# Moving half of the retention's projections beside the scans, a new order of the block inverses, and tokens loaded first

## The chip, the cores and the metric

The kernel runs on one core of one Trainium2 chip. The metric is the device time of one execution in microseconds (us). PE is TensorE (its weight loads are listed apart as PEld), DVE is VectorE, ACT is ScalarE, POOL is GpSimd; SP is SyncE, whose queue issues most of the DMA transfers.

## What is computed

Two transformer blocks follow each other on 1024 tokens of width 1024. Only the front of the first one is touched. There the tokens and 256 context tokens are normalised, modulated, and projected by `w_in` into two groups of columns: 2560 for a retention (q, k, v and two gates, 512 columns each) and 1920 for an RWKV part (r, k, v and low-rank terms). Cut to what matters:

```python
h = rms_norm(x, g_pre_mix) * (1.0 + sc1) + sh1
hc = rms_norm(ctx, g_pre_mix) * (1.0 + csc1) + csh1
u, uc = h @ w_in, hc @ w_in
ret_lat, _ = retention_group(u[..., :RET_COLS], uc[..., :RET_COLS], need_ctx)
rw = depthwise_conv(u[..., RET_COLS:], conv_w)
rwkv_lat, _ = rwkv_group(rw, rwc, ...)          # rwkv7_scan, forward and backward
lat = jnp.concatenate([ret_lat, rwkv_lat], axis=-1) @ w_out
```

`rwkv7_scan` is a recurrence over tokens, S = S * w_t + (S a_t) b_t + v_t k_t. The kernel computes it by chunks of 64 tokens, which takes the inverse of a triangular 64x64 matrix for each chunk, head and direction.

## The kernel before, in words

Python code writes the instructions; a scheduler then orders them on each engine by program order and by when it expects them to be ready, before the kernel runs. So a later part of the program may run beside an earlier one as far as its buffers are free; on the chip each engine goes through its list in order.

`phase_mod` (L147) loads 8 MB of modulation weights in eight transfers (L169) and makes the modulation columns (L171 to L181). `phase_h` (L227) loads the ten token tiles of 128 (L238), in groups of 4, 4 and 2, normalises them (L239, L240), transposes them on PE (L245), modulates them (L250, L252) and splits them in a high and a low part, hTh and hTl (L255, L256).

`phase_in` (L264) makes everything that the scans and the retention read, and writes it to DRAM. `project` (L326) gives the units of one block of 128 RWKV columns: up to three, by 512, 512 and 256 tokens, each with 24 matmuls; its result goes to Ud (L344). `retained` (L347) gives the units of 256 retention columns: one for each two token tiles, with 48 matmuls of 256 columns, whose result is stored in RD (L363). Each matmul is done three times, high by high, high by low and low by high (`mm3`, L106). `Weights.piece` (L74) loads a piece of weights (L90) and splits it on ACT (L91) and DVE or POOL (L92). The list `cols` (L566) holds the ten retained blocks: k, v, q and two gates f and b, for the first half of the heads and then for the second.

For each of four pairs of heads and for three token blocks, `prep` (L382) convolves r, k, v and builds the factors FA, FB and the triangular matrix L, which it stores in Ld (L500). The loop at L570 sets `prep` off in stages and puts projection units between the stages: those of the next pair, and of `cols` 0, 1, 2 to 3 and 4 to 6 for the four pairs. `tri(g)` (L502) inverts the 32x32 diagonal blocks of 128 matrices at once, one in each partition, row by row from the last: a product on DVE (L515) and a sum along the rows (L517). It is called for pair p-1 while pair p is prepared, for the context matrices (g = 4) in the last pair, and for pair 3 behind the loop (L598). The results go to Td (L524). Behind it stand the units of `cols` 7 to 9 (L599).

`phase_chain` (L603) does the scans: for each pair five groups, one of context chunks and four of latent chunks; a group does four chunks in each direction. For each direction come the scores (L684, L694), two sets of transposes (L701, L705), small products (L712, L713, L722, L731), two larger ones (L739, L752) and GQ (L757). Then four steps carry the state S (L777, L781, L786). Results are stored in Yd (L799). It reads some 24 tiles a group through SP. `phase_retention` (L828), with buffers from `ret_setup` (L802), does for each half of the heads some preparation (KV) and eight token blocks, whose results go to LatD (L932). Each second token block is followed by a part of `phase_mod2` (L184), which loads weights through POOL (L199) and sums on DVE (L203, L205). `phase_out` (L937) begins with the gates and the weights `w_out`.

The loop of units and preparations, and the end of phase_in:

```python
cols = [retained(*a, hh) for hh in range(2) for a in (("k", 512, 10), ...)]
for p in range(NPAIR):
    fill = pair(p + 1) if p < 3 else []
    for c in cols[(0, 1, 2, 4)[p]:(1, 2, 4, 7)[p]]:
        fill += c
    ...
W.lo_pool = True
tri(3)
for f in cols[7] + cols[8] + cols[9]:
    f()
```

Of the kernel before, what the change touches and what calls it, by code (L numbers as in the profile page):

```python
# [16 lines left out]
OP = mybir.AluOpType  # L17
# [129 lines left out]
def phase_mod(E, A):  # L147
# [8 lines left out]
    with tc.tile_pool(name="modp", bufs=1) as pool, tc.tile_pool(name="modps", bufs=1, space=PSUM) as pp:  # L156
# [7 lines left out]
        nc.vector.tensor_copy(E.cs.rearrange("p a k -> p (a k)"), cps[:, :2 * KD])  # L164
        rows = pool.tile([2, 4, 512], F32, name="modrows")
        ps = pp.tile([P, 512], F32, name="modps")
# [60 lines left out]
def phase_h(E, A):  # L227

    nc, tc = E.nc, E.tc
    E.hTh = E.hpool.tile([P, KD, TA], F32R, name="hTh")  # L230
    E.hTl = E.hpool.tile([P, KD, TA], F32R, name="hTl")
    with tc.tile_pool(name="php", bufs=3, side="right") as pool, tc.tile_pool(name="phps", bufs=3, space=PSUM, side="right") as pp:
        for g0, gn in ((0, 4), (4, 4), (8, 2)):
            xs = []
            for t in range(g0, g0 + gn):
                x = pool.tile([P, D], F32, tag="x", bufs=8, name=f"xin{t}")
                src = A.x[0, t * P:(t + 1) * P, :] if t < 8 else A.ctx[0, (t - 8) * P:(t - 7) * P, :]
                nc.sync.dma_start(x, src)  # L238
                r = row_norm(E, pool, x, f"n1_{t}")  # L239
                nc.vector.tensor_scalar(x, x, r, None, op0=OP.mult)  # L240
                xs.append(x)
            for k in range(KD):
                ps = pp.tile([P, 512], F32, tag="tp", name=f"htp{g0}_{k}")
                for i, x in enumerate(xs):
                    nc.tensor.transpose(ps[:, i * P:(i + 1) * P], x[:, k * P:(k + 1) * P], E.ident)  # L245
                n = gn * P
                c = 0 if g0 < 8 else 1
                f = pool.tile([P, 512], F32, tag="hf", name=f"hf{g0}_{k}")
                if k % 3 == 2:
                    nc.scalar.activation(f[:, :n], ps[:, :n], AF.Identity, scale=E.s1[:, k, c:c + 1], bias=E.mod[:, k, c:c + 1])  # L250
                else:
                    nc.vector.tensor_scalar(f[:, :n], ps[:, :n], E.s1[:, k, c:c + 1], E.mod[:, k, c:c + 1],  # L252
                                            op0=OP.mult, op1=OP.add)
                hi, lo = (a[:, k, g0 * P:g0 * P + n] for a in (E.hTh, E.hTl))
                nc.scalar.copy(hi, f[:, :n])  # L255
                (nc.vector if k % 2 else nc.gpsimd).tensor_sub(lo, f[:, :n], hi)  # L256
# [6 lines left out]

def phase_in(E, A):  # L264

# [8 lines left out]
                     (A.rwkv_a0, A.rwkv_k_k, A.rwkv_k_a, A.rwkv_r_k)])  # L274
    W0F, W0B, A0, KK, KA, RK = (lambda p, o=o: vec[:, o + p:o + p + 1] for o in (0, 4, 8, 12, 16, 20))
# [13 lines left out]
    Ud = [dt(f"Ud{m}", [P, TA + 4]) for m in range(16)]  # L289
# [3 lines left out]
    with ExitStack() as st:  # L293
        wp = st.enter_context(tc.tile_pool(name="inW", bufs=1))
        ep = st.enter_context(tc.tile_pool(name="inE", bufs=3))
        up = st.enter_context(tc.tile_pool(name="inU", bufs=1))
        tp = st.enter_context(tc.tile_pool(name="inT", bufs=1))
        rp = st.enter_context(tc.tile_pool(name="inR", bufs=1))
        pp = st.enter_context(tc.tile_pool(name="inP", bufs=4, space=PSUM))
        p2 = st.enter_context(tc.tile_pool(name="inQ", bufs=3, space=PSUM))  # L300
        W = Weights(E, wp, "inW", 128, 4, 3, 5)
# [24 lines left out]
        def project(m, blks):  # L326

            hold = []

            def unit(bi):  # L330
                if not hold:
                    hold.extend(W.full(w_in[:, R0 + CONV_COLS[m]:R0 + CONV_COLS[m] + P], P))
                t0, n, _ = TBLK[bi]
                ps = pp.tile([P, 512], F32, tag="pj", name=f"u{m}_ps{bi}")
                for k in range(KD):
                    mm3(nc, ps[:, :n], hold[k][0], hold[k][1], E.hTh[:, k, t0:t0 + n], E.hTl[:, k, t0:t0 + n], k == 0, k == KD - 1)
                ev = ep.tile([P, 514], F32, tag="ev", name=f"u{m}_{bi}")
                o = 0 if bi == 1 else 1
                w = n + (2 if bi == 2 else 1)
                for z in ((0,), (512,), (0, 257))[bi]:  # L340
                    nc.gpsimd.memset(ev[:, z:z + 1], 0.0)
                nc.scalar.copy(ev[:, o:o + n], ps[:, :n])  # L342
                d0 = (0, 513, 1026)[bi]
                nc.sync.dma_start(Ud[m][:, d0:d0 + w], ev[:, :w])  # L344
            return [lambda bi=bi: unit(bi) for bi in blks]

        def retained(n_, col, nt, hh):  # L347
# [4 lines left out]
            def unit(t0):  # L352
                if not hold:
                    hold.extend(W.full(w_in[:, col + c0:col + c0 + 256], 256, kper=2))
                ps = pp.tile([P, 512], F32, tag="pj", name=f"R{n_}{hh}_{t0}")
# [146 lines left out]
        def tri(g):  # L502
# [32 lines left out]

        for m, blks in ((12, (0, 1, 2)), (13, (0, 1, 2))):
            for f in project(m, blks):
                f()
# [31 lines left out]
        for p in range(NPAIR):  # L570
# [3 lines left out]
            for c in cols[(0, 1, 2, 4)[p]:(1, 2, 4, 7)[p]]:  # L574
                fill += c
# [23 lines left out]
        for f in cols[7] + cols[8] + cols[9]:  # L599
            f()  # L600


def phase_chain(E, A):  # L603
# [5 lines left out]
    with ExitStack() as st:  # L609
        ld = st.enter_context(tc.tile_pool(name="chL", bufs=2))  # L610
        wk = st.enter_context(tc.tile_pool(name="chW", bufs=2))
        cst = st.enter_context(tc.tile_pool(name="chC", bufs=1))
        ps_sc = st.enter_context(tc.tile_pool(name="chS", bufs=1, space=PSUM))
        ps_tr = st.enter_context(tc.tile_pool(name="chT", bufs=1, space=PSUM))
        ps_md = st.enter_context(tc.tile_pool(name="chM", bufs=2, space=PSUM))
        ps_ch = st.enter_context(tc.tile_pool(name="chX", bufs=2, space=PSUM))
        msk = cst.tile([P, 2, 2, 2, C], F32, name="scmask")
        nc.sync.dma_start(msk, E.consts["scmask"])

        PT4 = cst.tile([P, NPAIR, 20, 2, 2], F32, name="PT4")  # L620
        nc.vector.memset(PT4, 0.0)
        for p in range(NPAIR):
            for d in range(2):
                nc.vector.tensor_copy(PT4[0:64, p, :, d, 0], E.PT[0:64, p, d, :])
                nc.vector.tensor_copy(PT4[64:128, p, :, d, 1], E.PT[64:128, p, d, :])

        FAs = [cst.tile([P, G, 4, C], F32, name=f"FAb{i}") for i in range(4)]
        for t in FAs:
            nc.gpsimd.memset(t, 0.0)
        IRs = [cst.tile([P, G, 2, C], F32, name=f"IRb{i}") for i in range(4)]  # L630
        for t in IRs:
            nc.vector.tensor_copy(t[0:64, :, 0, :], E.ident[0:64, 0:64].unsqueeze(1).to_broadcast([64, G, C]))
            nc.vector.tensor_copy(t[64:128, :, 1, :], E.ident[64:128, 64:128].unsqueeze(1).to_broadcast([64, G, C]))

        TDs = [cst.tile([P, G, 2, C], F32, name=f"TDb{i}") for i in range(4)]
        for t in TDs:
            nc.gpsimd.memset(t, 0.0)
# [1772 lines left out]
def first(E, A):  # L2410
# [118 lines left out]
```

## Time and profile before

| | us |
|---|---|
| median of three runs | 4141.37 |
| lowest, highest | 4128.83, 4142.38 |
| the profiled execution | 4133.8 |
| its span, first to last instruction | 4132.0 |
| PE busy with matmuls | 3779.7 (91%) |
| PE busy with weight loads | 3133.2 (76%) |
| DVE busy | 2814.2 (68%) |
| ACT busy | 2127.7 (51%) |
| POOL busy | 825.2 (20%) |

The profiled execution lies between the runs. The stretch that the change touches is the first 1260 us; what follows is the output projection, the experts and the second block. A share over the whole span is a mean over stages with different limits, so the sections below go by stages.

### The profile page before, as it was taken

How to read it: one execution, taken by the hardware profiler on the slowest of the kernel's cores; microseconds unless marked ns; L12 is line 12 of the kernel's file. 1: busy time of each engine (PE TensorE's matmuls, PEld its weight loads, DVE VectorE, ACT ScalarE, POOL GpSimd, SP SyncE). 2: the span in 40 equal slices, each digit the busy share in tenths (PEclk: the TensorE clock that was granted, in tenths of full speed). 3: DMA queues.
4: the chain of work that ended last, by engine and by line, in shares of the span. 5: the costliest groups of instructions: out<-in, count | busy, mean ns of one | idle time of the engine just before them, and what ended most of it. 6: DMA issues, size and time to landing. Idle time of an engine off the chain costs nothing. (4 is left out here: it accounts for less than half of the span.)

```text
span 4132.0 us, 61749 instructions
## 1 busy us (share of the span) xinstructions
PE 3779.7 (91%) x23138; PEld 3133.2 (76%) x23138; DVE 2814.2 (68%) x4777; ACT 2127.7 (51%) x3389; POOL 825.2 (20%) x1054
## 2 busy tenths in 40 slices
PE   7988887998997879999969999999998999999998
PEld 4877886777875647777747788888886777788876
DVE  3578787776776578888865513676644356799987
ACT  3443322332323347777758712666653244688876
POOL 2333324233224120000010001222210022221111
PEclk7999998998998989999989999999999999899999
DMA  6555455455445379999851122111115425899998
GB/s 229 169 168 163 138 153 142 109 135 129 112 115 177 129 295 374 382 371 385 319 171 46 50 66 66 44 37 42 47 62 167 142 79 204 324 384 386 382 381 303
DMA packets 503961, 782.78 MB, mean 189 GB/s; under 512 B 199697, under 2 KB 334811, under 8 KB 502507
## 3 DMA queue, kind: packets, MB, share of 16 engines
q1 hardware_dynamic: 430314, 631.77, 43.8%
q0 software_dynamic: 40816, 138.37, 11.3%
q10 hardware_dynamic: 32528, 8.66, 0.9%
q8 instruction: 184, 3.01, 0.3%
q14 instruction: 119, 0.97, 0.1%
HBM read 646.28 MB, written 132.43 MB: 188 GB/s over the span
## 5 line engine op out<-in xcount | busy, mean ns | idle before, releaser
L2262 DVE TENSOR_TENSOR m2l<-m2r,m2h 128x1024 fp32r<-128x1024 f32 x380 | 449.6, 1222 | 53.0 <-ACT m2h L2261 48.6
L1195 DVE TENSOR_TENSOR m1l<-m1r,m1h 128x2048 fp32r<-128x2048 f32 x189 | 427.2, 2289 | 72.5 <-ACT m1h L1194 70.6
L2261 ACT CAST m2h<-m2r 128x1024 fp32r<-128x1024 f32 x384 | 394.0, 1050 | 86.5 <-PE m2g L109 34.6
L1194 ACT CAST m1h<-m1r 128x2048 fp32r<-128x2048 f32 x192 | 362.1, 1914 | 111.3 <-PE gu L109 82.6
L108 PE MATMUL m2g<-m2l,m2thx 128*128 128x512 f32 x512 | 202.7, 396 | 1.8 <-DVE m2l L2262 1.3
L107 PE MATMUL m2g<-m2h,m2thx 128*128 128x512 f32 x512 | 202.9, 405 | 0.3 <-ACT m2h L2261 0.3
L109 PE MATMUL m2g<-m2h,m2tlx 128*128 128x512 f32 x512 | 201.5, 394 | 0.0
L108 PE MATMUL gu<-m1l,xh 128*128 128x512 f32 x512 | 199.7, 395 | 0.0
L109 PE MATMUL gu<-m1h,xl 128*128 128x512 f32 x512 | 199.1, 395 | 0.0
L107 PE MATMUL gu<-m1h,xh 128*128 128x512 f32 x512 | 182.4, 397 | 12.7 <-ACT xh L60 8.3
L515 DVE TENSOR_TENSOR tripr<-triN,triX 128x1 f32<-128x1 f32 (+30 forms) x155 | 131.9, 851 | 19.5 <-POOL triX L511 15.9
L107 PE MATMUL apqk<-atW_hi,hT2h 128*128 128x256 f32 x512 | 145.1, 283 | 0.0
L108 PE MATMUL apqk<-atW_lo,hT2h 128*128 128x256 f32 x512 | 144.7, 283 | 0.0
L109 PE MATMUL apqk<-atW_hi,hT2l 128*128 128x256 f32 x512 | 144.7, 283 | 0.0
L107 PE MATMUL u_ps<-hTh,inW_hi 128*128 128x512 f32 (+1 forms) x336 | 127.1, 378 | 2.6 <-ACT u L342 1.5
L2314 POOL DMA_INDIRECT out_dram<-m2y,did x32 | 68.9, 2154 | 302.5 <-ACT m2y L2313 302.5
L108 PE MATMUL u_ps<-hTl,inW_hi 128*128 128x512 f32 (+1 forms) x336 | 124.4, 370 | 0.0
L109 PE MATMUL u_ps<-hTh,inW_lo 128*128 128x512 f32 (+1 forms) x336 | 124.1, 370 | 0.0
L107 PEld LDWEIGHTS gu<-m1h,xh 128*128 128x128 f32 x512 | 95.0, 188 | 37.0 <-ACT xh L60 10.7
L108 PEld LDWEIGHTS gu<-m1l,xh 128*128 128x128 f32 x512 | 96.4, 188 | 27.0 <-DVE m1l L1195 7.4
L1216 POOL DMA_INDIRECT accd<-y,idx x16 | 29.1, 1819 | 435.2 <-ACT y L1215 400.1
L108 PEld LDWEIGHTS m2g<-m2l,m2thx 128*128 128x128 f32 x512 | 96.8, 189 | 24.8 <-DVE m2l L2262 6.1
(1215 smaller groups left out, 11720.3 us busy)
## 6 DMA issues: line engine op xcount, KB each, us to landing
m2r<-in_w_gate_up_dram SPq DMA_DIRECT2D x128, 1024.0 KB
m1r<-in_w_gate_dram SPq DMA_DIRECT2D x64, 1024.0 KB
m1r<-in_w_up_dram SPq DMA_DIRECT2D x64, 1024.0 KB
m1r<-in_w_down_dram SPq DMA_DIRECT2D x64, 1024.0 KB
m2r<-in_w_down_dram SPq DMA_DIRECT2D x64, 1024.0 KB
inW_raw<-in_w_in_dram SPq DMA_DIRECT2D x72, 256.0 KB
m2w<-in_w_mod_dram POOLq DMA_DIRECT2D x32, 512.0 KB, 4.7
luW_raw<-in_w_in_dram SPq DMA_DIRECT2D x24, 512.0 KB
```

The source lines that it names most:

```text
L107: nc.tensor.matmul(ps, lh, rh, start=start, stop=False)
L108: nc.tensor.matmul(ps, lh, rl, start=False, stop=False)
L109: nc.tensor.matmul(ps, ll, rh, start=False, stop=stop)
L515: nc.vector.tensor_mul(pr[:, :m, :m], N[:, j, j + 1:].unsqueeze(1).to_broadcast([P, m, m]), X[:, j + 1:, j + 1:].rearrange("p s t -> p t s"))
L1194: nc.scalar.copy(hi, raw)
L1195: (nc.gpsimd if i < 3 else nc.vector).tensor_sub(lo, raw, hi)
L1216: nc.gpsimd.indirect_dma_start(out=E.accd, out_offset=bass.IndirectOffsetOnAxis(ap=E.idx[:, e:e + 1], axis=0), in_=y, in_offset=None, comp ...
L2261: nc.scalar.copy(hi, raw[:, j])
L2262: (nc.gpsimd if i in (0, 2) else nc.vector).tensor_sub(lo, raw[:, j], hi)
L2314: nc.gpsimd.indirect_dma_start(out=E.x4d, out_offset=bass.IndirectOffsetOnAxis(ap=col, axis=0), in_=y, in_offset=None, compute_op=OP.add)
```

## The change

The tokens are loaded and normalised by a class `Tokens` in three separate steps, and a new function `start` sets their order: the first group's loads stand ahead of the modulation's weights, the weights of the projections 12 and 13 ahead of the second group's loads, and the blocks of these projections between the token groups.

`tri` goes by columns instead of rows: for each column s from the last it multiplies column s of N with row s of X (an outer product) and adds it to the rows above.

The last pair's preparation gets only `cols[4]` beside it. The units of `cols` 5 to 9 (22 of them, the second half of the heads) are returned by `phase_in`, and `first` puts two of them behind each of the first eleven groups of the scans. For this `phase_chain` becomes a generator. Pools are laid on two sides of the memory, so that the scans' buffers and those of the projections are there at once; the projections have two PSUM buffers (inP2) in that time instead of four. The retention's buffers follow when the eleven groups are written.

```diff
+def start(E, A):
+    with tc.tile_pool(name="php", bufs=3, side="right") as pool, tc.tile_pool(name="phps", bufs=3, space=PSUM, side="right") as pp:
+        h = Tokens(E, A, pool, pp)
+        phase_mod(E, A, lambda: h.load(0))
+        low = [E.in_project(m, (None, 0, 1, 2)) for m in (12, 13)]
+        for u in low:
+            u[0]()
+        h.load(1)
+        h.norm(0)
+        h.turn(0)
+        h.load(2)
+        h.norm(1)
+        h.turn(1)
+        for u in low:
+            u[1]()
+        h.norm(2)
+        h.turn(2)
+        for u in low:
+            u[2]()
+            u[3]()
...
-            for j in range(B - 2, -1, -1):
-                m = B - 1 - j
-                pr = rp.tile([P, B - 1, B - 1], F32, tag="tP", name=f"tripr{g}_{j}")
-                nc.vector.tensor_mul(pr[:, :m, :m], N[:, j, j + 1:].unsqueeze(1).to_broadcast([P, m, m]),
-                                     X[:, j + 1:, j + 1:].rearrange("p s t -> p t s"))
-                nc.vector.tensor_reduce(X[:, j, j + 1:], pr[:, :m, :m], axis=AX.X, op=OP.add)
+            for s in range(B - 1, 0, -1):
+                m = B - s
+                pr = rp.tile([P, 16 * 16], F32, tag="tP", name=f"tripr{g}_{s}")[:, :s * m].rearrange("p (j t) -> p j t", t=m)
+                nc.vector.tensor_mul(pr, N[:, :s, s:s + 1].to_broadcast([P, s, m]),
+                                     X[:, s:s + 1, s:].to_broadcast([P, s, m]))
+                nc.vector.tensor_add(X[:, :s, s:], X[:, :s, s:], pr)
...
-        for m, blks in ((12, (0, 1, 2)), (13, (0, 1, 2))):
-            for f in project(m, blks):
-                f()
...
-            for c in cols[(0, 1, 2, 4)[p]:(1, 2, 4, 7)[p]]:
+            for c in cols[(0, 1, 2, 4)[p]:(1, 2, 4, 5)[p]]:
                 fill += c
...
         W.lo_pool = True
         tri(3)
-        for f in cols[7] + cols[8] + cols[9]:
-            f()
+        return sum(cols[5:], [])
...
+                yield
+    return run()
...
-        with tc.tile_pool(name="hp", bufs=1) as E.hpool:
-            with tc.tile_pool(name="pssm", bufs=1, space=PSUM) as E.ps_small:
-                phase_mod(E, A)
-                phase_h(E, A)
-                phase_in(E, A)
+        with ExitStack() as st:
...
+            start(E, A)
+            last = phase_in(E, A)
+            wide.close()
+            E.in_pools = E.in_pools[:2] + (ent(tc.tile_pool(name="inP2", bufs=2, space=PSUM, side="right")),)
+            cs = ExitStack()
+            run = phase_chain(E, A, cs)
+            for i, f in enumerate(last):
+                if i % 2 == 0:
+                    next(run)
+                f()
         with ExitStack() as E.rst:
-            E.rps = E.rst.enter_context(tc.tile_pool(name="reP", bufs=2, space=PSUM))
+            E.rps = E.rst.enter_context(tc.tile_pool(name="reP", bufs=2, space=PSUM, side="right"))
             tabs = ret_setup(E)
-            phase_chain(E, A)
+            for _ in run:
+                pass
+            cs.close()
             phase_retention(E, A, tabs, phase_mod2(E, A))
```

## Rows read from the trace of the kernel before

**Rows 1.** Windows by stage: PE, PEld, DVE, ACT, POOL busy, granted clock, DMA.
```profile
256.00:370.00 114.00, 102.70 (x717) 86.89 (x716) 94.24 (x156) 40.51 (x76) 43.14 (x71) 0.96 0.54 159
370.00:478.00 108.00, 96.28 (x749) 85.63 (x748) 86.14 (x146) 36.11 (x62) 36.58 (x54) 0.94 0.54 160
478.00:609.00 131.00, 109.97 (x935) 102.97 (x935) 119.25 (x198) 35.22 (x61) 41.26 (x51) 0.91 0.44 131
609.00:697.00 88.00, 67.32 (x541) 66.31 (x539) 63.61 (x99) 15.69 (x22) 26.70 (x29) 0.92 0.55 143
697.00:1260.00 563.00, 514.19 (x5257) 422.70 (x5257) 394.30 (x1041) 172.20 (x456) 175.80 (x229) 0.91 0.49 124
```

**Rows 2.** Windows for the tile tripr alone (the inverses): DVE busy, clock, DMA.
```profile
478.00:609.00 131.00, 79.27 (x121) 0.91 0.44 131
...
sum 441.00, DVE 209.55; mean DVE 52.39
```

**Rows 3.** Waits of PE and DVE, 256 to 609 us: total, times, longest.
```profile
PE ssi L438 <- DVE invb L433: 21.8, 5, 6.2
...
DVE L L492 <- PE psl L490: 19.0, 4, 13.5
```

**Rows 4.** Window with projections alone on PE, columns as in rows 1.
```profile
600.00:650.00 50.00, 50.00 (x419) 50.00 (x418) 38.44 (x55) 12.70 (x19) 14.05 (x13) 1.00 0.67 172
```

**Rows 5.** Timeline of SP and PE from the last projections to the scans.
```profile
636.37 38.63 SPq L363 DMA_DIRECT2D RDf<-Ref  x4
...
685.65 0.58 SPq L660 DMA_DIRECT2D FAb<-FA  x1
...
697.27 1.09 PE L857 MATMUL kTp<-ident,kt 128*128 128x128 f32 x4 [15.10 <-issue]
...
707.38 1.86 PE L694 MATMUL psc<-FAb,FB 128*128 128x128 f32 x7
```

**Rows 6.** Stores of the scans (Yd) and the retention (LatD): first and last.
```profile
L799 SPq DMA_DIRECT2D Yd<-yst x32: 320/378/716, 770.5 to 1256.2; - x32
L932 POOL DMA_DIRECT2D LatD<-gs x16: 582/619/635, 766.8 to 1243.5; - x16
```

**Rows 7.** Timeline of PE in one latent group of the scans.
```profile
1159.78 1.11 PE L739 MATMUL pw<-AT,TDb 128*128 128x128 f32 x8
1161.78 1.09 PE L752 MATMUL pg<-UT,W 64*64 64x128 f32 x16 [0.23 <-ACT W L741]
...
1165.26 0.59 PE L684 MATMUL psc<-FAb,FB 128*128 128x256 f32 x2
1165.69 0.38 PE L777 MATMUL pc<-S,GQ 128*128 128x128 f32 x2
...
1166.31 0.44 PE L777 MATMUL pc<-S,GQ 128*128 128x128 f32 x2
```

**Rows 8.** Timeline at the start: token loads, last modulation vector, first projection.
```profile
17.43 8.00 SPq L238 DMA_DIRECT2D xin<-in_x_dram  x8
30.59 0.17 DVE L181 SCALAR_TENSOR_TENSOR s<-s,c 128x16 f32<-128x16 f32 x1
64.94 0.77 PE L107 MATMUL u_ps<-hTh,inW_hi 128*128 128x512 f32 x1
```

**Rows 9.** Groups of DVE by form, 95 to 690 us: busy us, mean ns.
```profile
L470 DVE TENSOR_TENSOR FBt<-ic,ei 128x512 f32<-128x512 f32 x16 | 11.0, 685 | 0.0
L515 DVE TENSOR_TENSOR tripr<-triN,triX 128x961 f32<-128x961 f32 x5 | 9.6, 1926 | 0.1
L517 DVE TENSOR_REDUCE triX<-tripr 128x31 f32<-128x961 f32 x5 | 5.8, 1153 | 0.1
L470 DVE TENSOR_TENSOR FBt<-ic,ei 128x256 f32<-128x256 f32 x8 | 3.3, 418 | 0.0
```

**Rows 10.** Waits of PE's weight loads, 1254 to 1420 us.
```profile
PEld mo L107 <- ACT wohi L1047: 7.9, 2, 5.6
```

**Rows 11.** Waits, 1100 to 1260 us.
```profile
POOL m2w L199 <- DVE m2a L203: 29.1, 6, 11.8
```

More of the change, by code (lines that the diff above doesn't have):

```diff
@@ L144, in setup, with phase_mod @@
     nc.vector.memset(E.ones_col, 1.0)
-def phase_mod(E, A):
+def phase_mod(E, A, rows_first):
     nc, tc = E.nc, E.tc
@@ L155, in phase_mod @@
                              A.norm_gains[0, 0].rearrange("(r p) -> r p", p=P)])
-    with tc.tile_pool(name="modp", bufs=1) as pool, tc.tile_pool(name="modps", bufs=1, space=PSUM) as pp:
+    with tc.tile_pool(name="modp", bufs=1) as pool:
         crow = pool.tile([2 * KD, P], F32, name="crow")
@@ L164, in phase_mod @@
         nc.vector.tensor_copy(E.cs.rearrange("p a k -> p (a k)"), cps[:, :2 * KD])
+        rows_first()
         rows = pool.tile([2, 4, 512], F32, name="modrows")
-        ps = pp.tile([P, 512], F32, name="modps")
+        ps = E.in_pools[2].tile([P, 512], F32, tag="pj", name="modps")
         for k in range(KD):
@@ L224, in bc_row @@
     return t
[L227 to L256, printed above, removed]
@@ new lines, with __init__, load, norm @@
+class Tokens:
+    GROUPS = ((0, 4), (4, 4), (8, 2))
+    def __init__(self, E, A, pool, pp):
+        self.E, self.A, self.pool, self.pp = E, A, pool, pp
+        E.hTh = E.hpool.tile([P, KD, TA], F32R, name="hTh")
+        E.hTl = E.hpool.tile([P, KD, TA], F32R, name="hTl")
+        self.xs = {}
+    def load(self, g):
+        A, (g0, gn) = self.A, self.GROUPS[g]
+        for t in range(g0, g0 + gn):
+            x = self.xs[t] = self.pool.tile([P, D], F32, tag="x", bufs=8, name=f"xin{t}")
+            src = A.x[0, t * P:(t + 1) * P, :] if t < 8 else A.ctx[0, (t - 8) * P:(t - 7) * P, :]
+            self.E.nc.sync.dma_start(x, src)
+    def norm(self, g):
+        g0, gn = self.GROUPS[g]
+        for t in range(g0, g0 + gn):
+            x = self.xs[t]
+            r = row_norm(self.E, self.pool, x, f"n1_{t}")
+            self.E.nc.vector.tensor_scalar(x, x, r, None, op0=OP.mult)
+    def turn(self, g):
+        E, nc, pool = self.E, self.E.nc, self.pool
+        g0, gn = self.GROUPS[g]
+        for k in range(KD):
+            ps = self.pp.tile([P, 512], F32, tag="tp", name=f"htp{g0}_{k}")
+            for i in range(gn):
+                nc.tensor.transpose(ps[:, i * P:(i + 1) * P], self.xs[g0 + i][:, k * P:(k + 1) * P], E.ident)
+            n = gn * P
+            c = 0 if g0 < 8 else 1
+            f = pool.tile([P, 512], F32, tag="hf", name=f"hf{g0}_{k}")
+            if k % 3 == 2:
+                nc.scalar.activation(f[:, :n], ps[:, :n], AF.Identity, scale=E.s1[:, k, c:c + 1], bias=E.mod[:, k, c:c + 1])
+            else:
+                nc.vector.tensor_scalar(f[:, :n], ps[:, :n], E.s1[:, k, c:c + 1], E.mod[:, k, c:c + 1],
+                                        op0=OP.mult, op1=OP.add)
+            hi, lo = (a[:, k, g0 * P:g0 * P + n] for a in (E.hTh, E.hTl))
+            nc.scalar.copy(hi, f[:, :n])
+            (nc.vector if k % 2 else nc.gpsimd).tensor_sub(lo, f[:, :n], hi)
@@ L261, with in_project, project, unit @@
 CONV_COLS = [0, 128, 256, 384, 512, 640, 768, 896, 1024, 1152, 1280, 1408, 1536, 1600, 1728, 1856]
+def in_project(E, A, pools):
+    nc = E.nc
+    R0 = 2560
+    E.in_pools = wp, ep, pp = pools
+    E.Ud = [E.dram.tile([P, TA + 4], F32, name=f"Ud{m}") for m in range(16)]
+    E.in_W = W = Weights(E, wp, "inW", 128, 4, 3, 5)
+    def project(m, blks, hold=None):
+        hold = [] if hold is None else hold
+        def unit(bi):
+            if not hold:
+                hold.extend(W.full(A.w_in[0][:, R0 + CONV_COLS[m]:R0 + CONV_COLS[m] + P], P))
+            if bi is None:
+                return
+            t0, n, _ = TBLK[bi]
+            ps = pp.tile([P, 512], F32, tag="pj", name=f"u{m}_ps{bi}")
+            for k in range(KD):
+                mm3(nc, ps[:, :n], hold[k][0], hold[k][1], E.hTh[:, k, t0:t0 + n], E.hTl[:, k, t0:t0 + n], k == 0, k == KD - 1)
+            ev = ep.tile([P, 514], F32, tag="ev", name=f"u{m}_{bi}")
+            o = 0 if bi == 1 else 1
+            w = n + (2 if bi == 2 else 1)
+            for z in ((0,), (512,), (0, 257))[bi]:
+                nc.gpsimd.memset(ev[:, z:z + 1], 0.0)
+            nc.scalar.copy(ev[:, o:o + n], ps[:, :n])
+            d0 = (0, 513, 1026)[bi]
+            nc.sync.dma_start(E.Ud[m][:, d0:d0 + w], ev[:, :w])
+        return [lambda bi=bi: unit(bi) for bi in blks]
+    E.in_project = project
+def start(E, A):
+    nc, tc = E.nc, E.tc
+    with tc.tile_pool(name="php", bufs=3, side="right") as pool, tc.tile_pool(name="phps", bufs=3, space=PSUM, side="right") as pp:
[17 more added lines that the diff above has]
+            u[3]()
 def phase_in(E, A):
@@ L274, in phase_in @@
                      (A.rwkv_a0, A.rwkv_k_k, A.rwkv_k_a, A.rwkv_r_k)])
+    E.pss.close()
     W0F, W0B, A0, KK, KA, RK = (lambda p, o=o: vec[:, o + p:o + p + 1] for o in (0, 4, 8, 12, 16, 20))
@@ L288, in phase_in @@
     E.SGd = [dt(f"SGd{d}", [P, T]) for d in range(2)]
-    Ud = [dt(f"Ud{m}", [P, TA + 4]) for m in range(16)]
+    Ud = E.Ud
     E.RD = {n: dt(f"RD{n}", [TA if n in "kv" else T, 512]) for n in "qkvfb"}
@@ L293, in phase_in @@
     with ExitStack() as st:
-        wp = st.enter_context(tc.tile_pool(name="inW", bufs=1))
-        ep = st.enter_context(tc.tile_pool(name="inE", bufs=3))
+        wp, ep, pp = E.in_pools
         up = st.enter_context(tc.tile_pool(name="inU", bufs=1))
         tp = st.enter_context(tc.tile_pool(name="inT", bufs=1))
-        rp = st.enter_context(tc.tile_pool(name="inR", bufs=1))
-        pp = st.enter_context(tc.tile_pool(name="inP", bufs=4, space=PSUM))
+        rp = st.enter_context(tc.tile_pool(name="inR", bufs=1, side="right"))
         p2 = st.enter_context(tc.tile_pool(name="inQ", bufs=3, space=PSUM))
-        W = Weights(E, wp, "inW", 128, 4, 3, 5)
+        W, project = E.in_W, E.in_project
         lw = up.tile([P, 512], F32, name="lora_w2")
@@ L324, in phase_in @@
         AL = up.tile([P, TA], F32, name="AL")
[L326 to L345, printed above, removed]
         def retained(n_, col, nt, hh):
@@ L608, in phase_chain @@
     E.Yd = E.dram.tile([P, NPAIR, 2, 16, C], F32, name="Yd")
[L609 to L637, printed above, removed]
@@ new lines, in phase_chain @@
+    ld = st.enter_context(tc.tile_pool(name="chL", bufs=2))
+    wk = st.enter_context(tc.tile_pool(name="chW", bufs=2))
+    cst = st.enter_context(tc.tile_pool(name="chC", bufs=1))
+    ps_sc = st.enter_context(tc.tile_pool(name="chS", bufs=1, space=PSUM))
+    ps_tr = st.enter_context(tc.tile_pool(name="chT", bufs=1, space=PSUM))
+    ps_md = st.enter_context(tc.tile_pool(name="chM", bufs=2, space=PSUM))
+    ps_ch = st.enter_context(tc.tile_pool(name="chX", bufs=2, space=PSUM))
+    msk = cst.tile([P, 2, 2, 2, C], F32, name="scmask")
@@ new lines, in phase_chain @@
+    nc.sync.dma_start(msk, E.consts["scmask"])
+    PT4 = cst.tile([P, NPAIR, 20, 2, 2], F32, name="PT4")
+    nc.vector.memset(PT4, 0.0)
+    for p in range(NPAIR):
+        for d in range(2):
+            nc.vector.tensor_copy(PT4[0:64, p, :, d, 0], E.PT[0:64, p, d, :])
+            nc.vector.tensor_copy(PT4[64:128, p, :, d, 1], E.PT[64:128, p, d, :])
+    FAs = [cst.tile([P, G, 4, C], F32, name=f"FAb{i}") for i in range(4)]
+    for t in FAs:
+        nc.gpsimd.memset(t, 0.0)
+    IRs = [cst.tile([P, G, 2, C], F32, name=f"IRb{i}") for i in range(4)]
@@ L638, in phase_chain, with run @@
+    for t in IRs:
+        nc.vector.tensor_copy(t[0:64, :, 0, :], E.ident[0:64, 0:64].unsqueeze(1).to_broadcast([64, G, C]))
+        nc.vector.tensor_copy(t[64:128, :, 1, :], E.ident[64:128, 64:128].unsqueeze(1).to_broadcast([64, G, C]))
+    TDs = [cst.tile([P, G, 2, C], F32, name=f"TDb{i}") for i in range(4)]
+    for t in TDs:
+        nc.gpsimd.memset(t, 0.0)
+    def run():
         un = 0
```

11 lines of the change are left out of this document (9 added, 2 removed).

## The prediction

> **What bounds the kernel now.** I read the stretch that the change touches, the first 1260 us, by stages [rows 1], then what each stage waits for, then single durations. In the three stages where pairs 1 to 3 are prepared (256 to 370, 370 to 478, 478 to 609 us) the reader is to see DVE, not PE: it is busy 94.24 of 114, 86.14 of 108 and 119.25 of 131 us. Of that the block inverses alone take 79.27 in the third, and 209.55 us over all five, 42 each [rows 2]. PE's own wait there is for DVE: 21.8 us for invb [rows 3]. After 609 us come what is left of the retention's projections, dense on PE (50.00 of 50 us, 419 matmuls, so 119 ns each [rows 4]), then a gap of 15.1 us on PE and only at 707 us the first scores of the scans [rows 5]. From there the scans' 20 groups and the retention's 16 token blocks run side by side to 1256 and 1243.5 us [rows 6].
>
> That last stage has two readings. PE's matmul rows are busy 514.19 of 563 us, 91%; its weight loads are busy 422.70, 75% [rows 1], where the dense projections show 50.00 of 50 in both [rows 4]. So by matmuls there is room for 49 us of projections beside the scans, by weight loads for 140. I take the second: a pair of 256-column matmuls is drawn 0.59 us long, yet the next begins 0.43 later; overlapping tails fill the matmul row [rows 7]. The Trainium skill ("Perfetto Trace Analysis", Identifying the Most-Contended Engine) says the same: matmul busy share is no measure of PE's headroom, weight-load share is; by it the 125 us moved below would fit, by the other reading they would not, and that is a rival below. The trace agrees with it in the dense stretch.
>
> **The change, part by part.**
>
> *Start (tokens first).* Now the last modulation vector is ready at 30.6 us and the first projection starts at 64.94 [rows 8]. Afterwards four token tiles (2 MB) go ahead of the modulation's weights; eight took 8.00 us to issue, so the modulation comes 4 to 6 us later, but the first four norms are done under it, and the weights of the projections 12 and 13 and their block 0 no longer wait for the two other token groups. Their issues (4 weight loads, 6 stores) only move ahead on SP's queue, past the constants' small loads. Bounds 5 and 17 us, taken: 12 us gained, nearer the upper end since one whole token group (some 11 us of 35 for three) leaves the path.
>
> *Inverses.* Now 31 steps of a product and a sum over m x m, 42 us each. Afterwards 31 steps of a product and an addition over s(32-s) elements, 5456 in all instead of 10416. The longest old product took 1.93 us for 961 elements, read across rows, and its sum 1.15. Two-operand operations read along rows took 0.418 us at 256 elements and 0.685 at 512 [rows 9]: 0.151 us each plus 1.04 ns an element. So 2 x (31 x 0.151 + 5456 x 0.00104) = 20.7 us, five times 104 instead of 209.55. If the broadcast operand were as slow as the old product (1.85 ns an element), the product part would be 14.8 and all five 126. No row shows anything faster than the first value, so the saving is 84 to 106 us; I take 106, since the new operands run along rows.
>
> What of it shows: in the first two stages 20 us of DVE go from each, but PE's weight loads are 86.89 and 85.63 [rows 1], so they shrink to some 97 and 94, not below: 17 + 14. The third loses 2 x 20 and, its ten later projections being moved out, isn't held by PE: 131 to 91, 40 us. Sum 71, bounds 40 (PE and the chain of one preparation hold) and 85.
>
> *Projections beside the scans.* Twenty-two units (48 matmuls each, 22 x 48 x 0.119 = 125 us) leave the last preparation stage and the end. PE's price of a scan group: for each direction scores 4 x 0.43, three sets of eight 128-column matmuls 1.0 each (1.11 with the tail), packed sets 1.0 (1.09) and, for the smaller ones, 1.7; four state steps of 0.62 [rows 7]; together 9.9, of which I take 9.5, so 19 a group, and 11 for the three context groups, which skip half. Eleven groups: 8 x 19 + 3 x 11 = 185; with 125 this is 310 us. Five units (29 us) should run early, in PE's idle time of the third preparation stage, and three (17 us) in the 20 us in which the scans' buffers are set up and loaded (now 686 to 707 [rows 5]). That leaves 264, at 95% 278: the **first part** ends 298 us after the preparations. What hides the units is PE's 25%; without that cover they cost their full 125.
>
> Queues: SP gets 20 weight loads and 22 stores of 0.36 us, 16 us, between scan loads of 0.6 us, 24 a group; one blocked set of four stores has held SP for 38.63 us [rows 5], and scan loads behind such a store would be late, with UT and the state steps after them. POOL takes over 20 low halves; it is busy 175.80 of 563 [rows 1], so this is free.
>
> **Second part.** The retention's pools open only when the units are done, so it loses its company of eleven groups. Nine groups remain: now 16 latent and 4 context groups took 563 us, at 27 a latent group with a retention block; 8 x 27 + 19 = 235. In this time the retention, at its present pace (547 us for 16 blocks, 697 to 1243.5 [rows 6]), does 43%; 9.1 blocks' worth stay over. What a block costs alone isn't shown. Lower bound 11 (POOL's 175.80 / 16 [rows 1]), upper 34 (547 / 16); I take 16, close to the lower end, since no engine's own work is above it: 146 us. The second part is 235 + 146 = 381. While the retention ends alone, the output weights' split, for which mo waits 7.9 us [rows 10], is done early: 8 less.
>
> Sum behind the preparations: 298 + 381 - 8 = 671, now 1260 - 609 = 651: **20 lost**. Total: -12 - 71 + 20 = -63. The profiled execution took 4133.8 us (span 4132.0); 4133.8 - 63 = **4071**, I write 4070. That execution lies 7.6 below the median of 4141.4, inside the runs' 4128.8 to 4142.4.
>
> **Rivals.** About 0.3%, 12 us, is what the measurement can tell from no change.
>
> 1. *The retention's tail is as slow as now; slower than before.* POOL's queue, in order, waits for DVE before each load of the second modulation (29.1 us in 160, up to 11.8 at once [rows 11]); the norm's power and four transfers of each block stand behind it. If this, not the scans, sets the 34 us a block, the tail doesn't speed up. It loses the 63 us at 16 + 63 / 9.1 = 23 us a block; at 27 it is 9.1 x 11 = 100 worse: 4170. For it: 16 latent groups and 16 blocks, both halves at one pace. Against: no engine is near full with a block alone. 0.14.
> 2. *PE is full, as its matmul row has it.* The units then neither run early (+29) nor fill: 14 x 5.7 = 80 on groups of 27 without the retention's 4 of PE, 309 instead of 278 (+31): 4130, the same. For it: 91%. Against: weight loads at 75%. 0.17.
> 3. *The inverses were hidden.* The preparations are held by their own chain (DVE to PE and back), and 25 of 71 come: 4115. For it: DVE waited 19.0 us for psl [rows 3]. 0.12.
> 4. *More overlap.* Blocks alone at 11 (-45) and the first part at its floor of 250 (-28): 3996. 0.16.
> The forecast itself: 0.41.
>
> Slower: rival 1, 0.14. Within 0.3%: most of rival 2, 0.12. Faster: 0.74. The range leaves rival 1's own price and the far side of rival 4 out: 3995 to 4140.
>
> **What would show it.** Right: inverses at 20 to 25 us each; the last FB store before 540 us; PE's weight loads above 90% while units and groups alternate; then a stretch with retention alone, some 12 to 16 us a block. Wrong: preparations ending after 570; groups above 34 us with units; blocks alone above 23; or SP standing on a projection's store while scan loads wait behind it.

## The result, and the profile after

The changed kernel takes 4244.77 us (median of 4 runs, 4240.07 to 4256.84), the kernel before 4135.56 beside it: ratio 1.0267, 95% interval 1.0246 to 1.0288. It is **slower by 2.7%**, where 1.6% faster (4070 us) was forecast. The profiled execution took 4240.1 us (span 4238.3).

First the windows by stage of the changed kernel, columns as in [rows 1], cut where a stage really ends: the preparations of pairs 1 to 3, the gap up to the first scores, the eleven groups with units, the nine groups left, and the retention alone.

```profile
245.00:348.00 103.00, 92.07 (x656) 78.34 (x656) 71.76 (x149) 37.40 (x66) 37.69 (x62) 0.93 0.55 163
348.00:465.00 117.00, 108.26 (x806) 95.50 (x805) 75.74 (x156) 40.05 (x72) 37.11 (x63) 0.94 0.55 158
465.00:549.00 84.00, 72.87 (x599) 64.97 (x598) 70.98 (x135) 30.97 (x53) 41.06 (x52) 0.90 0.51 152
549.00:632.00 83.00, 67.13 (x500) 65.50 (x499) 53.89 (x131) 15.11 (x22) 19.55 (x23) 0.88 0.55 122
632.00:931.00 299.00, 280.33 (x2956) 238.09 (x2955) 130.57 (x391) 63.26 (x169) 14.58 (x24) 0.94 0.35 88
931.00:1177.00 246.00, 220.35 (x2299) 184.35 (x2299) 160.22 (x441) 75.25 (x204) 67.92 (x91) 0.92 0.48 122
1177.00:1365.00 188.00, 106.46 (x417) 80.70 (x416) 121.00 (x234) 49.21 (x104) 113.03 (x133) 0.51 0.41 124
```

The boundaries come from first and last starts of single transfers and matmuls of the changed kernel: stores of L, first scores, the last gate's projections, the loads of k for the retention, stores of the scans and of the retention (as [rows 6]).

```profile
L550 POOL DMA_DIRECT2D Ld<-L x48: 622/709/795, 151.8 to 548.6; - x48
L740 PE MATMUL psc<-FAb,FB x64: 270/275/415, 631.8 to 1042.0; 128*128 128x128 f32 x64
L413 SPq DMA_DIRECT2D RDb<-Reb x8: 360/366/394, 484.6 to 930.3; - x8
L898 POOL DMA_DIRECT2D kt<-RDk x2: 988/990/992, 931.5 to 1223.2; - x2
L845 SPq DMA_DIRECT2D Yd<-yst x32: 321/384/1245, 689.9 to 1176.7; - x32
L980 POOL DMA_DIRECT2D LatD<-gs x16: 570/586/618, 1085.0 to 1364.8; - x16
```

In the kernel before, the first scores came at 707.4 and the scans' and the retention's last stores at 1256.2 and 1243.5 [rows 5, 6]; the last L was stored at 598.9:

```profile
L500 POOL DMA_DIRECT2D Ld<-L x48: 624/707/800, 155.6 to 598.9; - x48
```

So everything up to the end of the scans is now 50 to 80 us earlier, and the retention's end is 121 us later. It starts only when the last unit is stored (930.3, its first load of k at 931.5), runs beside nine groups only, and its second half stands alone behind the scans: eight stores from 1280.8 to 1364.8, 12.0 us a block. In that last stage PE is busy 57% of the time at a granted clock of 0.51, about the lower of its two levels (1.2 GHz).

The inverses' own rows (windows from 252 to 645 us for the tile tripr alone, DVE) add up to this over all five, against 209.55 before [rows 2]:

```profile
sum 393.00, DVE 126.81; mean DVE 31.70
```

### The profile page after: what moved, and what is told of

It reads as the page before. It is cut to its first block, busy times and chain, and to the rows that moved or that the text cites. A ratio compares the mean times of both kernels' runs of the same rounds, so it can differ in the third digit from the quotient of the medians.

```text
span 4238.3 us, 61891 instructions
## 1 busy us (share of the span) xinstructions
PE 3834.5 (90%) x23138; PEld 3178.8 (75%) x23138; DVE 2732.4 (64%) x4769; ACT 2130.7 (50%) x3389; POOL 826.5 (20%) x1062
## 5 line engine op out<-in xcount | busy, mean ns | idle before, releaser
L1680 DVE TENSOR_SCALAR_CACHE_REDUCE pr<-sc 128x512 f32<-128x512 f32 (+2 forms) x192 | 103.6, 551 | 17.1 <-PE sc L1676 14.4
```

The lines of the kernel that those rows point to most:

```text
L1680: nc.vector.tensor_scalar(pr[:, m, n0:n1], ps[m][:, :n], -1.0, None, op0=OP.mult, op1=OP.min, accum_out=s[:, 4 * i + m:4 * i + m + 1])
```

## The experiments

Theory A was that the loss comes from the retention: it had run beside all 20 scan groups, and is now shut out of eleven. The rivals were the other parts of the change (B), the late start of the scans (C) and a PE that is full (D).

**e1: the units back before the scans**, all else as changed.

```diff
-            for c in cols[(0, 1, 2, 4)[p]:(1, 2, 4, 5)[p]]:
+            for c in cols[(0, 1, 2, 4)[p]:(1, 2, 4, 7)[p]]:
...
-        return sum(cols[5:], [])
+        for f in cols[7] + cols[8] + cols[9]:
+            f()
+        return []
```

> The changed kernel with one part undone: the 22 units stand before the scans again, three blocks beside the last preparation and three behind it; start, inverses and the sides of the pools stay as changed. Theory A (the loss comes from the retention, which is shut out while units stand beside the scans and so runs behind them): the retention runs beside the scans again and both end together some 50 to 70 us earlier than in the kernel before, 4065 to 4090 us. Rival B (the other parts, start, inverses and pools, cost the time or bring nothing): 4120 us or more.

Measured: 4153.75 us, 1.0049 (1.0032 to 1.0066). The move costs 2.2% of the 2.7%: in this A holds. But what stays of the change does not bring the gain that A expected of it (4065 to 4090); by the number this is B's case. The stores of scans and retention show where the gain went, and under them the window between their ends:

```profile
L847 SPq DMA_DIRECT2D Yd<-yst x32: 321/423/1536, 723.0 to 1196.2; - x32
L982 POOL DMA_DIRECT2D LatD<-gs x16: 558/611/640, 837.1 to 1269.5; - x16
```

```profile
1196.00:1270.00 74.00, 37.32 (x136) 28.75 (x136) 47.18 (x82) 21.69 (x41) 46.15 (x49) 0.54 0.52 152
```

The scans end 60 us earlier than before, the retention 26 later. The retention's first load of k, before and in e1:

```profile
L850 POOL DMA_DIRECT2D kt<-RDk x2: 969/973/977, 603.1 to 951.7; - x2
L900 POOL DMA_DIRECT2D kt<-RDk x2: 992/1000/1007, 668.3 to 1034.3; - x2
```

It comes 65 us later than before, while the first scores come 41 us earlier (666.2). So the scans now go first and the retention lags; its last 74 us are alone, on a PE at 0.54. The gain was given back there (e10 below gets it back). That the two sides of the memory make the retention late is likely, but no run tries it by itself.

**e2: four units a group**, `i % 4` for `i % 2` in `first`.

> The changed kernel with four units behind each of the first six groups instead of two behind each of eleven. Theory A: the last unit and with it the retention's buffers come three to five groups (70 to 120 us) earlier, and three to five blocks of some 12 us leave the tail: 4165 to 4210 us. Rival D (PE is full while units stand beside scans, so that packing them closer slows the scans by as much): within 15 us of the changed kernel, 4230 to 4260.

Measured: 4182.54 us, 1.0120 (1.0101 to 1.0139). Last gate and retention:

```profile
L413 SPq DMA_DIRECT2D RDb<-Reb x8: 360/366/376, 483.6 to 821.4; - x8
L980 POOL DMA_DIRECT2D LatD<-gs x16: 573/594/625, 966.0 to 1302.7; - x16
```

The last unit is stored at 821.4 instead of 930.3 and the retention ends at 1302.7 instead of 1364.8: 62 us for 109 of earlier opening, as A has it. D (4230 to 4260) falls.

**e3: no unit ahead of the scans**; each weight load of a unit waits for the first group's load of inverses.

```diff
+            if self.after is not None:
+                load_after(E, d, self.after)
...
+                if i == 0:
+                    E.in_W.after = E.td_load
```

> The changed kernel with every weight load of the 22 units held until the first scan group's inverses are loaded, so that no unit can go ahead of the scans. Theory C (the late start of the scans, 86 us behind the preparations instead of 20, is made by the units' loads, splits and stores ahead of the scans' on SP and POOL, and is most of the loss): scans start near 610 us and the time falls by 35 to 60 us, 4185 to 4210. Theory A: the last unit, and with it the retention, comes at about the same time as before (some 920 to 960 us), so the scans' earlier end only makes the tail longer: 4225 to 4270.

Measured: 4293.65 us, 1.0386 (1.0368 to 1.0403), 49 us worse than the change, more than either theory said. Scores, last gate and retention:

```profile
L743 PE MATMUL psc<-FAb,FB x64: 270/275/582, 613.4 to 1083.5; 128*128 128x128 f32 x64
L416 SPq DMA_DIRECT2D RDb<-Reb x8: 360/360/377, 480.6 to 984.7; - x8
L983 POOL DMA_DIRECT2D LatD<-gs x16: 571/583/618, 1150.6 to 1419.4; - x16
```

The scans start 18 us earlier, the last unit is 54 later, and the end follows the last unit. C falls: even without a unit in the way the first scores come 75 us behind the last L (538.2). POOL's timeline of this run shows what stands there:

```profile
577.26 0.95 POOL L563 MEMSET triX<- 128x1024 f32 x1 [29.85 <-DMA Td<-triX]
...
608.55 3.63 POOL L677 MEMSET FAb<- 128x1024 f32 x4 [30.13 <-DMA Td<-triXT]
612.10 1.95 POOL L685 MEMSET TDb<- 128x512 f32 x4
```

Two inverses, one behind the other because X has one buffer (its next filling waits until the last X is stored in Td), and only behind them the scans' buffers. From the first scores to the last unit, eleven groups with all 22 units beside them, two to a group, took:

```profile
613.00:985.00 372.00, 366.06 (x3571) 321.51 (x3572) 131.66 (x395) 78.45 (x193) 31.00 (x38) 0.93 0.35 91
```

**e5 and e4: the inverses by themselves.** e5 is the kernel before with the new loop of `tri` alone, e4 the changed kernel with the old one.

> The kernel before with only the inverses by outer products. As on record the inverses cost 42 us each and 23 to 31 by the changed trace. Theory A with the inverses worth what they save where DVE holds a stage: PE's ten late projections stay in the third stage, so 25 to 50 us of it come: 4085 to 4110 us. Rival (the inverses were hidden): 4125 to 4140 us.

> The changed kernel with the old inverses, by rows. In the kernel before, the new inverses alone changed nothing that can be measured (1.0009), though they took 96 us off DVE, since PE's projections filled the time. In the changed kernel the third preparation stage has lost its ten late projections. Theory A with a stage that DVE holds: the preparations end 25 to 40 us later and so do the scans, the last unit and the retention: 4265 to 4285 us. Rival (the inverses are hidden there too): 4235 to 4255.

Measured: e5 4136.75 us, 1.0009 (0.9996 to 1.0021); e4 4279.05, 1.0341 (1.0324 to 1.0358), 34 us above the change. So in the kernel before the inverses were hidden, and in the changed kernel they are not. Windows of e5, the last preparation and what follows it, and then its sum for tripr alone:

```profile
478.00:582.00 104.00, 92.79 (x826) 86.38 (x826) 86.25 (x199) 32.56 (x57) 33.44 (x46) 0.98 0.51 149
582.00:680.00 98.00, 82.73 (x650) 80.86 (x648) 23.82 (x68) 18.35 (x27) 20.57 (x22) 0.91 0.48 132
```

```profile
sum 393.00, DVE 113.65; mean DVE 28.41
```

DVE lost 96 us and the last L came 17 us earlier (582.0), but the units behind it still end at 680, as before (682.9), and the scans' buffers wait for them, as POOL's timeline of e5 shows:

```profile
678.97 3.84 POOL L630 MEMSET FAb<- 128x1024 f32 x4 [21.20 <-PE Rb L109]
```

So of the 96 us 13 reached the first scores (694.4), and none the end: the last stores of scans and retention came at 1250.3 and 1249.7. In e4 the last L and the first scores were:

```profile
L550 POOL DMA_DIRECT2D Ld<-L x48: 624/709/814, 150.8 to 560.5; - x48
L739 PE MATMUL psc<-FAb,FB x64: 270/275/582, 683.5 to 1101.7; 128*128 128x128 f32 x64
```

Against the changed kernel the old inverses cost 12 us up to the last L and 52 up to the first scores: most of what the new ones gain is gained behind the preparations, where two of them stand in series.

**e8 and e9: the retention written ahead of the scans**, in e1 and in the changed kernel.

```diff
+            phase_retention(E, A, tabs, phase_mod2(E, A))
             for _ in run:
                 pass
             cs.close()
-            phase_retention(E, A, tabs, phase_mod2(E, A))
```

> The kernel with the units back before the scans, and the retention written ahead of the scans, so that it goes first wherever both are ready. With the units back and the retention behind, the retention was the later one: its last store came at 1280 us, the scans' at 1207. Theory G (that order, and not PE's work, sets the end): the retention ends by some 1000 us, the scans are the later ones with 8 to 10 groups alone at 23 us, and end at 1220 to 1270: 4110 to 4155. Rival (the retention cannot go faster than 27 us a block): it ends near 1200 again and the time is within 15 us of 4154.

> The changed kernel with the retention written ahead of the nine groups that are left when it starts. Theory A (what is lost is the retention's tail alone behind the scans, 188 us on a PE at half clock): retention and scans now end together near 1260 to 1310 instead of 1375: 4125 to 4185 us. Rival F (a late retention costs the same wherever its blocks stand, since beside the scans each slows the other): 4230 to 4260.

Measured: e8 4266.31 us, 1.0303 (1.0277 to 1.0329); e9 4232.36, 1.0228 (1.0211 to 1.0245). Theory and rival of e8 both missed: it is by far the worse order. Its stores of scans and retention, and then two windows: the retention's, with its two preparations and three groups of the scans (one of context, two latent), and that of the 14 latent and 3 context groups left:

```profile
L847 SPq DMA_DIRECT2D Yd<-yst x32: 320/380/1255, 864.4 to 1392.5; - x32
L982 POOL DMA_DIRECT2D LatD<-gs x16: 557/586/634, 731.4 to 974.1; - x16
```

```profile
670.00:974.00 304.00, 219.97 (x1407) 172.05 (x1406) 202.84 (x476) 85.82 (x208) 170.21 (x214) 0.68 0.45 129
974.00:1393.00 419.00, 374.96 (x3842) 306.11 (x3843) 197.74 (x573) 85.64 (x246) 10.68 (x21) 0.84 0.33 83
```

The groups alone cost 419 / 17 = 24.6 us each. Context groups are no shorter: the three stretches of one context and one latent group, between stores of Yd, took 40, 56 and 54 us. The retention's 304 us hold three groups, so alone it takes between 304 - 3 x 24.6 = 230 and 304. In e9 the retention ends at 1247.9 and the scans at 1365.1: the tail has changed its owner and the end is the same (1364.8 in the changed kernel), as F said.

**e10: in turns.** e1 with the retention as a generator: its preparation, then one step behind each group.

```diff
+            ret = phase_retention(E, A, tabs, phase_mod2(E, A))
+            next(ret)
             for _ in run:
-                pass
+                next(ret, None)
             cs.close()
-            phase_retention(E, A, tabs, phase_mod2(E, A))
+            for _ in ret:
+                pass
```

> The kernel with the units back before the scans, and the retention written in turns with the scans: its preparation first, then a block or the second preparation behind each scan group. Theory G (the 20 us that the units-back kernel loses against the kernel before come from the order of scans and retention alone): both end together near 1235 to 1255 us, the last unit's 12 us of gain are seen, 4105 to 4130 us. Rival (the pools on two sides or the start cost it elsewhere): 4145 to 4160.

Measured: **4088.91 us**, 0.9885 (0.9869 to 0.9902), faster than both kernels and below what G expected. Its stores:

```profile
L847 SPq DMA_DIRECT2D Yd<-yst x32: 320/424/1564, 753.5 to 1210.9; - x32
L983 POOL DMA_DIRECT2D LatD<-gs x16: 558/605/625, 733.0 to 1142.1; - x16
```

From the first scores (665.3) to 1210.9 all 20 groups and the retention take 546 us. In e8, for the most part one behind the other, they took 723 (670 to 1393): 177 more, which is also the difference of the two kernels' times. If the retention alone took the whole 304, the sum alone would be 304 + 20 x 24.6 = 796, 250 more. So side by side hides 177 to 250 us, 9 to 12.5 a group.

**e13 and e14: which part brings it.** e13 is the kernel before with the turns alone, e14 is e10 with the old inverses.

> The kernel before with nothing changed but the retention written in turns with the scans. There scans and retention already end together (1267 and 1254 us). Theory G' (the order is worth nothing there; the 47 us that the units-back kernel in turns gains come from start, pools and inverses): 4125 to 4140. Rival (the order alone brings it, by fewer waits and a better filled PE): 4085 to 4110.

> The units-back kernel in turns with the old inverses. Theory (PE's projections hold the time up to the last unit, at 678 us, so the inverses are hidden): 4083 to 4100 us, as with the new ones (4089). Rival (with PE's work in order the 20 us an inverse show): 4105 to 4130.

Measured: e13 4111.77 us, 0.9943 (0.9924 to 0.9961); e14 4096.29, 0.9911 (0.9892 to 0.9929). The order alone brings 0.6%, which G' did not expect and which is just short of what its rival said; start and pools about 0.3% more and the inverses 0.3% more. The last two steps are as small as the intervals, so how the rest divides between them is open.

**e11 and e12: the units moved, in turns.** The changed kernel with two steps of the retention behind each of the nine groups, and e2 with 19 steps over 14 groups.

> The changed kernel with the retention written in turns with the nine groups left, two steps of it behind each. With the retention ahead of everything it ran some 300 us alone and the scans followed alone, to 1376 us again. Theory A (what counts is how long the two stand side by side; alone the retention needs 300 us and nine groups some 210): with both side by side from 941 us they end near 1250 to 1300, 4125 to 4185 us, still well above the 4089 of the units-back kernel in turns, where the retention has all 20 groups. Rival F (a late retention costs the same whatever the order): 4225 to 4255.

> Four units behind each of the first six groups, and the retention in turns with the 14 groups left. Theory A: 14 groups at some 27 us from 835 us, and both end at 1215 to 1245: 4080 to 4125 us, the same as or behind the units-back kernel in turns (4089), so that units beside the scans bring nothing even then. Rival H (units beside scans are worth their 80 to 125 us once the retention is in order): 4030 to 4070.

Measured: e11 4213.33 us, 1.0193 (1.0175 to 1.0211); e12 4151.63, 1.0036 (1.0018 to 1.0054). With the order mended the move still costs 124 and 63 us against e10, more than A had reckoned; e11 lies between A and F. A window of e11 (from its last unit on, nine groups with the whole retention) and one of e12 (six groups with ten units):

```profile
945.00:1319.00 374.00, 306.89 (x2719) 245.58 (x2718) 266.20 (x669) 115.20 (x299) 173.20 (x220) 0.86 0.51 132
```

```profile
632.00:822.00 190.00, 185.06 (x1827) 158.21 (x1827) 73.78 (x224) 38.58 (x97) 13.46 (x20) 0.92 0.34 88
```

Two steps of the retention beside a group stretch it to 374 / 9 = 42 us. Six groups (148 alone) with ten units (57 by the price of the prediction) take 190: 148 + 57 - 190 = 15 us hidden, 2.5 a group.

**e15 and e16: four or eight units moved, in turns**, behind the first one or two groups. By then it was open whether any unit beside the scans can win (L) or whether that brings nothing (K).

> The units-back kernel in turns with only the last four units (gate b, second half of the heads) moved, behind the first scan group. Theory K (the scans hide a fixed amount of other work a group and the retention uses it up): the scans start some 20 us earlier, but the retention too has to wait for the units and the two end together no earlier: 4085 to 4100 us. Rival L (only a late retention costs; few units beside the context group win their own price of 5.9 us each): 4062 to 4075.

> The same with the last eight units (both gates, second half of the heads), four behind each of the first two scan groups. Theory K: 4088 to 4110 us, no better than with four and on the way to the 4152 of 22 units. Rival L: 4040 to 4065.

Measured: e15 4084.96 us, 0.9877 (0.9844 to 0.9909); e16 4093.15, 0.9891 (0.9859 to 0.9922). Both the same as e10. Scores and stores of the retention, e15 and then e16:

```profile
L742 PE MATMUL psc<-FAb,FB x64: 270/275/377, 645.9 to 1087.0; 128*128 128x128 f32 x64
L983 POOL DMA_DIRECT2D LatD<-gs x16: 563/596/645, 759.2 to 1163.1; - x16
```

```profile
L742 PE MATMUL psc<-FAb,FB x64: 275/275/582, 626.2 to 1093.4; 128*128 128x128 f32 x64
L983 POOL DMA_DIRECT2D LatD<-gs x16: 563/600/624, 794.6 to 1189.6; - x16
```

The scans start 19 and 39 us earlier than in e10 (665.3), and end no earlier (1210.3 and 1222.1 against 1210.9). In e10 the retention was done 69 us ahead of the scans, here 47 and 33. So up to eight moved units cost nothing, but they win nothing either: the times are K's, not L's.

## Why the prediction was wrong

By its steps, the profiled execution against the sum (us):

| step | forecast | measured | miss |
|---|---|---|---|
| end of the preparations (last L) | -83 | 598.9 to 548.6: -50 | +33 |
| from there to the first scores | 20 | 83 | +63 |
| eleven groups with units | 278 | 299 | +21 |
| nine groups | 235 | 246 | +11 |
| retention alone | 146 | 188 | +42 |
| output projection, behind it | -8 | 175.9 to 169.5: -6 | +2 |

Together 172; 4240.1 missed 4071 by 169. The last row goes from the last store to the last copy of the output projection (tile mix). The sum counts from its stage ends, 609 and 1260, the table from last stores, 598.9 and 1256.2, so rows can shift by up to 10 us against each other.

**The step that failed** is the cost of the first part, "that leaves 264, at 95% 278: the first part ends 298 us after the preparations"; it ended 382 behind the last L. Two things were wrong in it.

The 264 took PE for a queue that work fills to 95%, and reckoned the eleven groups as 185 us of its work. The scans are a chain: alone, with nothing beside them, they take 24.6 us a group (e8), so eleven take 271. Their windows in e8 show how it looked like room: weight loads 306 of 419 us, 73%, matmul rows 375, 89%. Ten units beside eleven groups came to 299, so 271 + 57 - 299 = 29 us of them were hidden, half, and PE's weight loads stood at 238 of 299, 80%, not above 90%. In e3, with 22 units, it is 271 + 126 - 372 = 25. (e8's scans ran at a granted clock of 0.84, these stretches at 0.94 and 0.93, so the 271 is an estimate.)

The reading that the prediction left to rival 2 fits better: the matmul row of the bare scans leaves 10.5% free, which is 28 us of 271 (29 and 25 were hidden) and 16 of e12's 148 (15). Whether this share holds in other chains no run here shows.

The Trainium skill ("Perfetto Trace Analysis", Identifying the Most-Contended Engine) has PE's headroom judged by FLOP utilisation and weight-load share instead of matmul busy share. The trace differs here: of the 27% that weight loads leave free in the bare scans, only about 10 could be filled.

The 20 was a stage that had only looked short because 14 units covered it: two inverses in series and the scans' buffers behind them (e3: 75 us without a unit). Twelve units, not eight, ran there and before (the eleventh and twelfth stored at 625); the other ten came beside the scans, the last eight of them beside the last groups, stored from 829 to 930.

**Second part.** "In this time the retention, at its present pace, does 43%" failed too: its first store came 154 us behind its first load (931.5 to 1085.0), and five blocks, not seven, were done by 1177. The price of a block alone was right in kind: 12.0 us against 16, and 34 as the upper bound. But a whole second preparation stood in the tail too: 188. The price of the nine groups came nearly true (246 for 235), though its parts do not add up to the stage that they were read from: 16 x 27 + 4 x 19 is 508, not 563.

**Preparations.** The inverses took 127 instead of 104, just above the other price given (126). 10 of these 23 us are there in e5 too (113.65), where each inverse took 22 to 23 us instead of 20.7; the other 13 are told at the end. The 71 us of theirs and the 12 of the start came as 50 together, and not from where the sum had them. The first two stages won nothing: pair 2's last L was stored at 465.5 instead of 467.5, although 35 us of inverses had left DVE by then. The third won 48, of which e4 gives the inverses 12. So DVE, which the prediction saw as what bounds the stages, did not hold the first two. The start: the first projection came 24 us earlier (40.88 against 64.94), but the first store of L only 4 (151.8 against 155.6); what holds it there was not looked into.

**The rivals.** Rival 1 forecast the right sign by a mechanism that does not act: blocks alone take 12 us, not 27. Rival 2, PE full, describes the part with units best (94% by the matmul row, 98% in e3) and missed what that does to the retention. Rival 3 is true of the kernel before (e5: no difference for 96 us of DVE) and not of the changed one (e4: 34 us), since there the units that hid them are gone. Rival 4's blocks nearly came (12.0 us against 11), its first part did not. None of the prediction's signs of being wrong came either: the preparations ended before 570, groups with units took 27 us (34 in e3), blocks alone 12, and the longest wait of SP for a unit's store beside the scans was 7.1 us. What no rival had is a budget: a scan group hides 9 to 12.5 us of the retention, work that lives on DVE, ACT and POOL and in waits, but only some 2.5 of dense projections. The change gave eleven of the 20 places to work that the scans cover badly, and turned out the work that they cover well.

## What to carry to other kernels

Before moving work beside a dependent chain, measure the chain alone and ask what the place holds now: an engine's idle share inside a chain, by weight loads above all, is not room for as much more work on that engine, and what is turned out of the place has to be paid alone. Where two chains share a stretch, write them in turns so that both end together; here that alone was worth 0.6%, and 1.1% with the rest of the change but without the move. A saving on an engine shows only if nothing else fills the same stretch: the same inverses were worth nothing with the units behind them and 34 us without.

## What the runs showed of the hardware

DVE's two-operand steps of the inverses took 0.40 to 0.43 us at 250 elements, and more than three times as long while POOL subtracted. Timeline of DVE and POOL in the changed kernel:

```profile
519.64 0.40 DVE L566 TENSOR_TENSOR tripr<-triN,triX 128x256 f32<-128x256 f32 x1
...
521.53 1.42 DVE L566 TENSOR_TENSOR tripr<-triN,triX 128x255 f32<-128x255 f32 x1
522.98 1.39 DVE L568 TENSOR_TENSOR triX<-triX,tripr 128x255 f32<-128x255 f32 x1
524.40 1.36 DVE L566 TENSOR_TENSOR tripr<-triN,triX 128x252 f32<-128x252 f32 x1
...
528.77 0.42 DVE L568 TENSOR_TENSOR triX<-triX,tripr 128x247 f32<-128x247 f32 x1
```

```profile
521.16 2.91 POOL L512 TENSOR_TENSOR sg<-cum,sg 128x512 f32<-128x512 f32 x2
524.04 2.85 POOL L92 TENSOR_TENSOR inW_lo<-inW_raw,inW_hi 128x512 fp32r<-128x512 f32 x2
```

Each DVE step then lasts about as long as one of POOL's (2.91 and 2.85 us for two). Of the inverses' 310 steps 20 took over 1 us in the changed kernel, 8 in e5; the 12 more make most of the 13 us above. The prediction had called the low halves on POOL free; here they were not, while DVE read two operands.

The Trainium skill ("SBUF — State Buffer", Who interferes with whom) says so: a VectorE instruction with two inputs in SBUF contends with a GpSimd instruction that reads SBUF, and the later one waits for the earlier to finish. The trace agrees, 0.42 us becoming about 1.4.

In a tail alone PE's granted clock was low as well: 0.51 in the changed kernel's last 188 us, 0.54 in e1's last 74 and 0.68 in the retention part of e8, against 0.92 where retention and scans stood side by side (e10, 665 to 1142). How much of a tail's length this makes was not separated.
